# Two-layer attention and retention encoder on one core: other planner constants, nine written page orders, and another pair of operands cut by seven

## The chip, the cores and the metric

The kernel runs on one core of a Trainium2 chip. The time is the device time of one execution in microseconds (us), and lower is better. The profile is of one execution; its times are counted from the first instruction.

## What is computed

Each of two layers normalises the residual stream, multiplies it with one wide input matrix, runs grouped-query attention on half of the heads and two-way retention on the other half, and multiplies both with one output matrix:

```
DEPTH = 2; SEQ = 256; D_MODEL = 4096; IN_WIDTH = 11264
for l in range(DEPTH):
    h = rmsnorm(x, norm_w[l])
    aq, ak, av, ag, rq, rk, rv, rg = split(h @ w_in[l])          # 4096 x 11264
    a_out = silu(ag) * gqa_attention(rope(rmsnorm(aq)), rope(rmsnorm(ak)), av)
    r_out = silu(rg) * rmsnorm(bidirectional_retention(rope(rq), rope(rk), rv))
    x = x + concat(a_out, r_out) @ w_out[l]                      # 4096 x 4096
return rmsnorm(x, final_norm)
```

All of it is float32. The weights, 4096 by 11264 and 4096 by 4096 numbers in each layer, are read once.

## The kernel before

**Blocks and pairs.** The two big products are made in 30 blocks of 1024 output columns, numbered here 0 to 29 in the order in which they run: 11 of the first product of layer 0 (blocks 0 to 10), 4 of its second product (11 to 14), and the same for layer 1 (15 to 25, 26 to 29). A block runs over 4096 input channels as 16 pairs of 256 channels. For each pair the operand (256 tokens) is a 2 by 2 block matrix and so are the weights. An "eight" pair multiplies all eight quarter products. A "seven" pair uses the seven products of a fast 2 by 2 scheme, with sums of weight quarters (tile `wsum`) and sums of operand quarters (tile `xf`).

**Three matmuls for a product.** Float32 is kept by splitting each number into two rounded parts: ACT casts a weight page to `whi`, DVE subtracts to get `wlo`; operands are split likewise into `x8h`, `x8l` (eight pairs) and `x7h`, `x7l` (seven pairs). A product is then three matmuls of 128 by 128 by 512: high by high, high by low, low by high. An eight pair so costs 24 matmuls, a seven pair 21. Pairs 0 and 1 of block 0 are multiplied unsplit.

**Pages.** The weights of an eight pair come as two pages, A and B, those of a seven pair as four, A, T, B and U (T and U are made of sums). Rings of four `whi` and four `wlo` buffers hold pages ahead of TensorE, and six `wraw` buffers hold raw weights, loaded by the SP queue. A "far" page is loaded by the GpSimd queue straight into `fhi`; ACT negates it into `flo`, and a second, accumulating transfer adds the weights to that, so that DVE has nothing to do for it. By `FAR_PAIRS` page B of pairs 3, 6, 9, 12 and 15 is far, where the pair is an eight; in block 0 only from the third seven pair on.

**Which pairs are sevens.** `SEVEN` are sevens throughout, `AFTER` names pairs that become sevens from some block of a product on, one number for each layer. A pair that turns from eight to seven gets the missing operand sums in `sevenfold`, made between its last use in one block and its first use in the next. In the first two blocks (`PLAIN`) an eight pair uses an eighth PSUM bank; the operand differences that later blocks need (`third`, tile `x3f`) are made during blocks 0 to 2.

**The planner.** The program is written by a planner that runs when the kernel is built. It keeps a model of each engine's time (`Model`, with costs for each operation and `LATE`, the time until another engine sees a result) and gives the next instruction of DVE and ACT to whichever work, among what the model has ready within 0.02 us, has the earliest deadline less its own duration. A weight page's deadline is the modelled moment of its first matmul less `SLACK`. Everything else (operand splits, attention, retention, residual) runs in `Lane`s: an operand split is due `REST` before its first use, and other lanes follow two constants:

```python
return max(self.due, at + self.soft) if self.soft == SOFT else at + self.soft
```

Here `at` is now, `SOFT` is 5 us and `self.due` is the moment of the lane's creation plus `DUE`, 90 us. Some late tasks have `soft=URGENT` (0) and ignore `DUE`. The matmuls of attention and retention (PSUM tile `ps`) are put between the block's matmuls by `aside` once the model has their inputs ready for `PE_REST`. Once written, each engine's stream is fixed and runs in order.

Of the kernel before, what the change touches and what calls it, by code (L numbers as in the profile page):

```python
# [17 lines left out]
P = 128  # L18
# [28 lines left out]
DUE = 90.0  # L47

SOFT = 5.0
# [7 lines left out]
REST = 6.0  # L57
# [11 lines left out]
SEVEN = (0, 2, 5, 8, 11, 13)  # L69
# [3 lines left out]
AFTER = ({10: (3, 1)}, {10: (1, 1)})  # L73
# [11 lines left out]
MIX = False  # L85

GATE = 1

FAR_GAP = 0.0

SHIFT = 0.5
# [91 lines left out]

def in_groups(sevens, first=False):

    order = []
    for group in [tuple(range(_a, _b)) for _a, _b in zip(sevens, sevens[1:] + (NP,))]:
        one, rest = group[:1], group[1:]
        if first:
            order += [(_p, _k) for _p in NATIVE if _p in group for _k in (PAGE_A, PAGE_B)]  # L190
            one = [_p for _p in one if _p not in NATIVE]
            rest = [_p for _p in rest if _p not in NATIVE]
        one = [(_p, _k) for _p in one for _k in (PAGE_A, PAGE_T, PAGE_B, PAGE_U)]
        rest = [(_p, _k) for _p in rest for _k in (PAGE_A, PAGE_B)]
        for _v in one:
            order += [_v] + rest[:1]
            rest = rest[1:]
        order += rest
    return order


def evenly(sevens):

    order = []
    for _kind in (True, False):
        pages = [
            (_p, _k)
            for _p in range(NP)
            if (_p in sevens) == _kind
            for _k in ((PAGE_A, PAGE_T, PAGE_B, PAGE_U) if _kind else (PAGE_A, PAGE_B))  # L210
        ]
        order += [((_i + (SHIFT if _kind else 0.5)) / len(pages), _v) for _i, _v in enumerate(pages)]
    return [_v for _, _v in sorted(order)]


def pages_of(sevens, first=False):

    return in_groups(sevens, first) if first or not MIX else evenly(sevens)


def slots_of(sevens, first=False, plain=False):

    for _p, _k in pages_of(sevens, first):
# [20 lines left out]
LATE = {"V": 0.137, "A": 0.152, "P": 0.223, "G": 0.15}  # L244
# [243 lines left out]
def hybrid_encoder(  # L488
# [79 lines left out]
    def plan_of(l, second, b):  # L568
# [3 lines left out]
        plan.phase = 2 * l + 1 + second  # L572
        plan.start = (l, second, b) == (0, 0, 0)
# [5 lines left out]
        for slot in slots_of(plan.sevens, plan.start, plan.plain):  # L579
            flat += slot  # L580
# [25 lines left out]
    taken = [0]  # L606
# [83 lines left out]
    class Weights:  # L690


        def __init__(self):
            self.pages, at, far_after = [], 0, 0.0
            for plan in plans:
# [3 lines left out]
                for n, (name, p, _, k, h) in enumerate(plan.flat):  # L699
                    if (p, k) not in made:  # L700
# [4 lines left out]
                        at_page = cum[at + n]  # L705
                        one.far = not one.seven and not (start and (p < plan.sevens[2] or one.whole))
                        if FAR_GAP:
                            one.far = one.far and at_page >= far_after
                        else:
                            one.far = one.far and k == PAGE_B and p in FAR_PAIRS  # L710
                        if one.far:
                            far_after = at_page + FAR_GAP
# [63 lines left out]
        def due(self, g, low=False):  # L776
            return model.free["P"] + cum[g.first] - cum[done[0]] + (2 * MM * g.run if low else 0.0) - SLACK
# [207 lines left out]
    def split_pair(p, v, whole, stage):  # L985
# [44 lines left out]
        else:  # L1030
# [22 lines left out]
            if stage in DEFER:  # L1053
                if late is None or late > PLAIN:
                    thirds.append(Lane(third(p, *u, g)))
                    thirds[-1].pair = p
                    thirds[-1].use = plans[PLAIN].begins + next(i for i, v in enumerate(plans[PLAIN].flat) if v[1] == p)
# [76 lines left out]
    class Turn:  # L1134
# [21 lines left out]
        def soon(self, c):  # L1156
            return cum[first_use[self.stage + 1][2 * c]] - cum[done[0]] < AHEAD
# [34 lines left out]

    class Lane:
        def __init__(self, steps, heavy=True, need=0, own=0, owner=None, due=None, soft=None):
            self.need, self.own, self.owner = need, own, owner
            self.soft = SOFT if soft is None else soft
            self.steps, self.ops, self.begun, self.ended, self.then = steps, [], False, False, None
            self.due = clock["V"] + DUE if due is None else due
# [28 lines left out]
        def rested(self, at):  # L1227
# [7 lines left out]
            return ready + PE_REST <= max(at, free)  # L1235
# [367 lines left out]
    def retention_weights(L, i):  # L1603

        L.making = True
# [45 lines left out]
        L.weights[i], L.making = wT, False  # L1651
# [118 lines left out]
    def block(plan, after_pair, combine, then):  # L1770

        flat, order, plain, second = plan.flat, plan.order, plan.plain, plan.second
        first_order, last = plan.start, plan.last
# [292 lines left out]
    for i, L in enumerate(layers):  # L2066
        L.index = i
        L.rstd, L.kept, L.making = None, False, False
# [56 lines left out]
    for plan in plans:  # L2125
        l, L = plan.layer, layers[plan.layer]
        if not plan.second:
            bi = plan.b
            one = BLOCKS[bi][0]
            if one[0] == "rg":  # L2130
                tasks.append(Lane(retention_weights(L, one[1]), False, 3))
                tasks[-1].gate = lambda L=L, i=one[1]: not L.weights and (GATE < 1 or i // 2 in L.stored) and (GATE < 2 or not L.making)
# [92 lines left out]
```

## Time and profile before

| | |
|---|---|
| time, median of 3 runs | 2583.06 us (2581.98 to 2584.73) |
| time of the profiled execution | 2582.32 us |
| its span, first to last instruction | 2580.6 us |
| TensorE matmul, busy | 2565.2 us (99%) |
| TensorE weight load, busy | 2122.7 us (82%) |
| DVE, busy | 2340.3 us (91%) |
| ACT, busy | 1696.1 us (66%) |
| transfers | 690.75 MB, 268 GB/s |

A matmul's end in the profile is modelled and overlaps the next one, so a short wait of TensorE does not show as idle time; it is read from the distance between the starts of successive matmuls. 1.7 us of the profiled execution lie outside the span.

### The profile page before, as it was taken

The numbers are of one execution on the slowest core, as the hardware profiler recorded it, in microseconds if no ns is written. First come the engines' busy times: TensorE is split into PE (matmuls) and PEld (weight loads), VectorE is DVE, ScalarE is ACT, GpSimd is POOL, SyncE is SP. The second block draws the span as 40 slices with busy tenths as digits, with TensorE's granted clock in tenths as the row PEclk, the third lists the DMA queues.
The fourth block names the chain that finished last, engine by engine and source line by source line (L and its number), as shares of the span: only waits on it lengthen the run. The fifth ranks groups of instructions, "written<-read, shape, count | busy, mean of one in ns | idle before, by whom it ended". The sixth has DMA issues, their size and how long they took to land.

```text
span 2580.6 us, 34258 instructions
## 1 busy us (share of the span) xinstructions
PE 2565.2 (99%) x11491; PEld 2122.7 (82%) x11491; DVE 2340.3 (91%) x2939; ACT 1696.1 (66%) x2431; POOL 479.4 (19%) x694
## 2 busy tenths in 40 slices
PE   9999999999999999999999999999999999999998
PEld 7888888888888888888888888888888888888886
DVE  7999999889989999888899989999899899998887
ACT  7766766656665768555786666766666666775565
POOL 0211312211122111211121113212122112111111
PEclk9999999999999999999999999999999999999999
DMA  9998888878878887998998889898887887888896
GB/s 321 312 280 271 273 266 291 271 250 278 247 234 266 239 278 247 286 285 244 324 304 268 258 255 305 256 282 269 259 275 244 243 265 235 274 253 260 266 269 204
DMA packets 203858, 690.75 MB, mean 268 GB/s; under 512 B 24736, under 2 KB 31392, under 8 KB 203680
## 3 DMA queue, kind: packets, MB, share of 16 engines
q1 hardware_dynamic: 126304, 443.14, 48.0%
q0 software_dynamic: 77376, 245.41, 37.9%
q8 instruction: 90, 1.47, 0.2%
q14 instruction: 88, 0.72, 0.1%
HBM read 641.27 MB, written 47.19 MB: 267 GB/s over the span
## 4 chain that ended last, share of the span: by engine, by line
PE 96%; DVE 2%; DMA 1%; issue 1%; ACT 0%; POOL 0%; DVEq 0%; POOLq 0%; SPq 0%; ACTq 0%
PE M L421 92%; PE ps L421 4%; DVE wlo L421 1%; DMA flo<-in_w_in 1%; DVE cb L421 0%; DMA p_dram<-room 0%; DVE ca L421 0%; DMA full<-in_xT 0%; DVE wsum L421 0%; ACT ps L421 0%; DVE x8l L421 0%; ACT ca L421 0%; ACT tanh L421 0%; POOL p_dram L421 0%; DVE pTl L421 0%
## 5 line engine op out<-in xcount | busy, mean ns | idle before, releaser
L421 ACT CAST whi<-wraw 128x1024 fp32r<-128x1024 f32 (+1 forms) x807 | 753.5, 937 | 340.0 <-PE M L421 296.8
L421 DVE TENSOR_TENSOR wlo<-wraw,whi 128x1024 fp32r<-128x1024 f32 (+1 forms) x807 | 862.5, 1078 | 74.7 <-ACT whi L421 65.2
L421 ACT CAST whi<-wsum 128x1024 fp32r<-128x1024 f32 x406 | 426.2, 1050 | 257.4 <-PE M L421 157.6
L421 DVE TENSOR_TENSOR wlo<-wsum,whi 128x1024 fp32r<-128x1024 f32 x406 | 494.8, 1219 | 97.4 <-ACT whi L421 70.4
L421 PE MATMUL M<-whi,x7h 128*128 128x512 f32 x1465 | 570.7, 390 | 0.1
L421 PE MATMUL M<-whi,x7l 128*128 128x512 f32 x1465 | 570.4, 389 | 0.0
L421 PE MATMUL M<-wlo,x7h 128*128 128x512 f32 x1465 | 476.2, 389 | 0.0
L421 PE MATMUL M<-whi,x8l 128*128 128x512 f32 x1153 | 448.9, 389 | 0.1
L421 PE MATMUL M<-whi,x8h 128*128 128x512 f32 x1153 | 448.9, 389 | 0.0
L421 PE MATMUL M<-wlo,x8h 128*128 128x512 f32 x1153 | 355.6, 389 | 0.0
L421 PEld LDWEIGHTS M<-wlo,x7h 128*128 128x128 f32 x1465 | 274.9, 188 | 57.5 <-DVE wlo L421 0.3
L421 PEld LDWEIGHTS M<-whi,x7h 128*128 128x128 f32 x1465 | 275.1, 188 | 56.8 <-DVE cb L421 0.5
L421 PEld LDWEIGHTS M<-whi,x7l 128*128 128x128 f32 x1465 | 275.2, 188 | 56.4 <-issue 0.2
L421 ACT ACTIVATE flo<-fhi 128x1024 fp32r<-128x1024 f32 (+1 forms) x149 | 156.7, 1052 | 171.6 <-PE M L421 164.5
L421 PEld LDWEIGHTS M<-whi,x8h 128*128 128x128 f32 x1153 | 216.5, 188 | 45.4 <-DVE ca L421 0.5
L421 PEld LDWEIGHTS M<-whi,x8l 128*128 128x128 f32 x1153 | 216.5, 188 | 45.4 <-DVE x8l L421 0.6
L421 PEld LDWEIGHTS M<-wlo,x8h 128*128 128x128 f32 x1153 | 216.5, 188 | 45.1
L421 DVE TENSOR_TENSOR wsum<-wraw 128x1024 f32<-128x1024 f32 x203 | 247.0, 1217 | 4.8 <-DMA wraw<-in_w_in 2.7
L421 PE MATMUL M<-whi,x 128*128 128x512 f32 x728 | 224.3, 389 | 0.0
L421 POOL DMA_DIRECT2D fhi<-in_w_in x109 | 60.6, 556 | 875.7 <-PE M L421 871.9
L421 PE MATMUL M<-fhi,x8l 128*128 128x512 f32 x441 | 171.7, 389 | 0.0
L421 PE MATMUL M<-fhi,x8h 128*128 128x512 f32 x441 | 171.6, 389 | 0.0
(268 smaller groups left out, 3193.4 us busy)
## 6 DMA issues: line engine op xcount, KB each, us to landing
wraw<-in_w_in SPq DMA_DIRECT2D x591, 512.0 KB, 6.0
wraw<-in_w_out SPq DMA_DIRECT2D x216, 512.0 KB, 6.0
fhi<-in_w_in POOLq DMA_DIRECT2D x109, 512.0 KB, 5.2
flo<-in_w_in POOLq DMA_DIRECT2D x109, 512.0 KB, 8.5
fhi<-in_w_out POOLq DMA_DIRECT2D x37, 512.0 KB, 5.2
flo<-in_w_out POOLq DMA_DIRECT2D x37, 512.0 KB, 8.2
full<-next_dram POOLq DMA_DIRECT2D x24, 512.0 KB, 8.5
p_dram<-room POOLq DMA_DIRECT2D x64, 128.0 KB, 5.5
```

The costliest lines, as they stand in the source:

```text
L421: op.call()
```

## The change

Pair 5 leaves `SEVEN` and is listed in `AFTER`: in layer 0's first product it is an eight in block 0 and a seven from block 1 on, elsewhere a seven throughout. Pair 10, so far a seven from block 3 on in layer 0's first product, is one from block 1 on. `DUE` goes from 90 to 0 and `SOFT` from 5 to 7, so that a lane without a use is always due 7 us from now; `REST` goes from 6 to 9; the model's `LATE` becomes smaller. In nine blocks the order of pages is read from a table, `ORDERS` (a number is the pair, the letter its page), in place of `in_groups`. `FARS` sets the far pages of blocks 0, 7 and 18: pair 6 in block 0 (and by the rule on the third seven pair only 9, 12 and 15 are left there), pair 15 in block 7 and pair 9 in block 18 are no longer far. `SETS` overrides `SLACK` or `SOFT` in blocks 0, 8 and 23. Choices that were switched off (`MIX`, `FAR_GAP`) are removed.

```diff
-DUE = 90.0
-SOFT = 5.0
+DUE = 0.0
+SOFT = 7.0
...
-REST = 6.0
+REST = 9.0
...
-SEVEN = (0, 2, 5, 8, 11, 13)
+SEVEN = (0, 2, 8, 11, 13)
 MORE = ()
-AFTER = ({10: (3, 1)}, {10: (1, 1)})
+AFTER = ({5: (1, 0), 10: (1, 1)}, {5: (0, 0), 10: (1, 1)})
...
+ORDERS = {
+    2: '0A 0T 1A 1B 0B 2A 3A 2T 0U 3B 2B 4A 2U 4B 5A 6A 5T 5B 6B 7A 5U 7B 8A 9A 8T 9B 8B 8U 10A 10T 10B 10U 11A 12A 11T 12B 11B 13A 14A 11U 13T 14B 13B 13U 15A 15B',
...
+    23: '0A 0T 1A 1B 0B 3A 0U 2A 2T 3B 2B 4A 2U 4B 6A 5A 5T 6B 5B 7A 5U 7B 8A 9A 8T 9B 8B 8U 10A 10T 10B 10U 11A 12A 11T 12B 11B 11U 13A 14A 13T 14B 13B 13U 15A 15B',
+}
+FARS = {
+    0: '3B 9B 12B 15B',
+    7: '3B 6B 9B 12B',
+    18: '3B 6B 12B 15B',
+}
+SETS = {
+    (0, 'SLACK'): 0.0,
+    (8, 'SOFT'): 5.0,
+    (23, 'SOFT'): 5.0,
+}
...
-LATE = {"V": 0.137, "A": 0.152, "P": 0.223, "G": 0.15}
+LATE = {"V": 0.11, "A": 0.112, "P": 0.198, "G": 0.15}
...
+        plan.index = l * (N_IN + N_OUT2) + second * N_IN + b
+        plan.fars = parsed(FARS[plan.index]) if plan.index in FARS else [(p, PAGE_B) for p in FAR_PAIRS]
...
+        pages = parsed(ORDERS[plan.index]) if plan.index in ORDERS else in_groups(plan.sevens, plan.start)
+        for slot in slots_of(pages, plan.sevens, plan.start, plan.plain):
...
         def deadline(self, at):
             if self.use is not None:
-                return model.free["P"] + cum[self.use] - cum[done[0]] - REST
-            return max(self.due, at + self.soft) if self.soft == SOFT else at + self.soft
+                return model.free["P"] + cum[self.use] - cum[done[0]] - setting("REST", REST)
+            if self.soft is None:
+                return max(self.due, at + setting("SOFT", SOFT))
+            return at + self.soft
```

`ORDERS` holds blocks 2, 3, 4, 8, 15, 18, 19, 22 and 23.

## Rows read from the trace of the kernel before

**Rows 1.** The page's head: busy us, share of the span and instructions of each engine.
```profile
PE 2565.2 (99%) x11491; PEld 2122.7 (82%) x11491; DVE 2340.3 (91%) x2939; ACT 1696.1 (66%) x2431; POOL 479.4 (19%) x694
```
**Rows 2.** The chain that ended last, in order of time: start, us, what.
```profile
173.99 63.92 PE M L421 x282
...
2048.28 92.51 PE M L421 x408
```
**Rows 3.** Timeline 17 to 31 us: start, us, instruction, idle before it and releaser.
```profile
19.49 0.79 PE L421 MATMUL M<-whi,x7h 128*128 128x512 f32 x1
...
20.12 0.40 PE L421 MATMUL M<-whi,x7l 128*128 128x512 f32 x1
...
28.81 0.39 PE L421 MATMUL M<-whi,x8h 128*128 128x512 f32 x1
...
29.34 0.19 PEld L421 LDWEIGHTS M<-whi,x8l 128*128 128x128 f32 x1 [0.57 <-DVE x8l L421]
```
**Rows 4.** Timeline 90 to 96 us, the turn from block 0 to block 1.
```profile
94.33 0.39 PE L421 MATMUL M<-wlo,x7h 128*128 128x512 f32 x1
...
94.81 0.19 PEld L421 LDWEIGHTS M<-whi,x7h 128*128 128x128 f32 x1 [0.52 <-DVE cb L421]
```
**Rows 5.** Timeline of PE, 611 to 613 us, early in block 7.
```profile
611.43 0.62 PE L421 MATMUL M<-whi,x 128*128 128x512 f32 x2
612.29 0.51 PE L421 MATMUL ps<-pTl,kv 128*128 128x512 f32 x1 [0.24 <-DVE pTl L421]
```
**Rows 6.** Timeline of PE, 975.5 to 978.5 us, in block 11.
```profile
975.96 0.28 PE L421 MATMUL ps<-vh,wTh 128*128 128x256 f32 x1
976.48 0.39 PE L421 MATMUL ps<-vl,wTh 128*128 128x256 f32 x1 [0.25 <-DVE vl L421]
976.71 0.28 PE L421 MATMUL ps<-vh,wTl 128*128 128x256 f32 x1
976.83 0.28 PE L421 MATMUL ps<-vh,wTh 128*128 128x256 f32 x1
...
977.37 0.28 PE L421 MATMUL ps<-vh,wTl 128*128 128x256 f32 x1
```
**Rows 7.** Timeline of PE, 1450.5 to 1453.5 us, late in block 16.
```profile
1450.95 0.61 PE L421 MATMUL M<-fhi,x 128*128 128x512 f32 x2
1452.93 0.50 PE L421 MATMUL M<-flo,x 128*128 128x512 f32 x1 [1.37 <-DMA flo<-in_w_in]
```
**Rows 8.** The accumulating transfers into flo: issue to landing, last line of that tile's view.
```profile
DMA to landing us min/median/max: 4.0/8.4/13.3
```
**Rows 9.** Blocks 0, 1, 2, 3, 7: stretch, length, busy us of each engine, clock, transfers.
```profile
6.00:93.20 87.20, 87.01 (x354) 66.36 (x355) 74.38 (x106) 72.05 (x129) 6.38 (x9) 1.00 0.98 345
93.20:176.50 83.30, 83.20 (x367) 68.62 (x366) 81.10 (x134) 53.31 (x79) 22.85 (x23) 1.00 0.95 285
176.50:261.70 85.20, 85.20 (x385) 70.87 (x385) 81.17 (x110) 55.71 (x85) 14.69 (x21) 1.00 0.84 260
261.70:349.10 87.40, 87.40 (x394) 72.56 (x393) 81.15 (x97) 59.84 (x93) 21.12 (x33) 1.00 0.89 283
...
609.10:696.30 87.20, 86.96 (x388) 71.76 (x388) 82.02 (x97) 54.62 (x65) 14.51 (x22) 1.00 0.83 251
```
**Rows 10.** DVE's groups in block 1: count, busy us, mean ns of one, idle before.
```profile
L421 DVE TENSOR_TENSOR wlo<-wraw,whi 128x1024 fp32r<-128x1024 f32 x21 | 25.3, 1214 | 0.0
...
L421 DVE TENSOR_TENSOR wsum<-wraw 128x1024 f32<-128x1024 f32 x6 | 7.3, 1214 | 0.0
L421 DVE TENSOR_TENSOR wsum<-wraw,wsum 128x512 f32<-128x512 f32 x7 | 4.8, 680 | 0.0
```
**Rows 11.** The operand sums, tile xf: duration ns min/median/max, first and last start.
```profile
L421 DVE TENSOR_TENSOR x7l<-xf,x7h x28: 806/815/826, 10.7 to 2312.8; 128x640 fp32r<-128x640 f32 x28
...
L421 DVE TENSOR_TENSOR xf<-full x24: 275/281/284, 9.4 to 2293.3; 128x128 f32<-128x128 f32 x24
...
L421 DVE TENSOR_TENSOR xf<-x7h,x7l x4: 681/683/684, 240.1 to 2306.8; 128x512 f32<-128x512 f32 x4
```

More of the change, by code (lines that the diff above doesn't have):

```diff
@@ L181, in sevens_of, with parsed @@
     return tuple(sorted({*SEVEN, *(MORE if second else ()), *late}))
+def parsed(text):
+    return [(int(_v[:-1]), "ATBU".index(_v[-1])) for _v in text.split()]
 def in_groups(sevens, first=False):
@@ L199, in in_groups, with slots_of @@
     return order
[L202 to L223, printed above, removed]
+def slots_of(order, sevens, first=False, plain=False):
+    for _p, _k in order:
         if _p in sevens and not (first and _p in NATIVE):
@@ L605, in hybrid_encoder @@
             cum.append(cum[-1] + MM * (WHOLE if plan.start and v[1] in NATIVE else 3))
-    taken = [0]
+    taken, playing = [0], [0]
     nw = t(cp, [P, DEPTH * (KT + KT // 2)], "nw")
@@ L693, in __init__ @@
         def __init__(self):
-            self.pages, at, far_after = [], 0, 0.0
+            self.pages, at = [], 0
             for plan in plans:
@@ L704, in __init__ @@
                         one.seven = p in plan.sevens and not one.whole
[L705 to L712, printed above, removed]
+                        one.far = (p, k) in plan.fars and not one.seven and not (start and (p < plan.sevens[2] or one.whole))
                         one.kept = None
@@ L776, in due @@
         def due(self, g, low=False):
-            return model.free["P"] + cum[g.first] - cum[done[0]] + (2 * MM * g.run if low else 0.0) - SLACK
+            return model.free["P"] + cum[g.first] - cum[done[0]] + (2 * MM * g.run if low else 0.0) - setting("SLACK", SLACK)
         def ready(self, e, ins, old=None):
@@ L1056, in split_pair @@
                     thirds[-1].pair = p
-                    thirds[-1].use = plans[PLAIN].begins + next(i for i, v in enumerate(plans[PLAIN].flat) if v[1] == p)
+                    plan = plans[stage // 2 * (N_IN + N_OUT2) + PLAIN]
+                    thirds[-1].use = plan.begins + next(i for i, v in enumerate(plan.flat) if v[1] == p)
             else:
@@ L1156, in soon @@
         def soon(self, c):
-            return cum[first_use[self.stage + 1][2 * c]] - cum[done[0]] < AHEAD
+            return cum[first_use[self.stage + 1][2 * c]] - cum[done[0]] < setting("AHEAD", AHEAD)
         def step(self):
@@ L1191, in free_bank, with setting @@
         do(partial(bank.__setitem__, 0, False))
+    def setting(name, value):
+        return SETS.get((playing[0], name), value)
     class Lane:
@@ L1195, in __init__ @@
             self.need, self.own, self.owner = need, own, owner
-            self.soft = SOFT if soft is None else soft
+            self.soft = soft
             self.steps, self.ops, self.begun, self.ended, self.then = steps, [], False, False, None
-            self.due = clock["V"] + DUE if due is None else due
+            self.due = clock["V"] + setting("DUE", DUE) if due is None else due
             self.pair = self.use = None
@@ L1234, in rested @@
             model.free["P"] = free
[L1235 removed]
+            return ready + setting("PE_REST", PE_REST) <= max(at, free)
         def deadline(self, at):
             if self.use is not None:
[L1239 to L1240 removed]
+                return model.free["P"] + cum[self.use] - cum[done[0]] - setting("REST", REST)
+            if self.soft is None:
+                return max(self.due, at + setting("SOFT", SOFT))
+            return at + self.soft
     def spawn(steps):
@@ L1650, in retention_weights @@
         yield
-        L.weights[i], L.making = wT, False
+        L.weights[i] = wT
         own(-2)
@@ L2067, in hybrid_encoder @@
         L.index = i
-        L.rstd, L.kept, L.making = None, False, False
+        L.rstd, L.kept = None, False
         L.tables, L.weights, L.rs, L.stored = {}, {}, {}, {}
@@ L2131, in hybrid_encoder @@
                 tasks.append(Lane(retention_weights(L, one[1]), False, 3))
-                tasks[-1].gate = lambda L=L, i=one[1]: not L.weights and (GATE < 1 or i // 2 in L.stored) and (GATE < 2 or not L.making)
+                tasks[-1].gate = lambda L=L, i=one[1]: not L.weights and i // 2 in L.stored
             if bi == N_IN - 1:
```

7 lines of the change are left out of this document (1 added, 6 removed), and 7 rows, old and new, of the table ORDERS.

## The prediction

> **What bounds the kernel now.** I read the head of the page first: TensorE's matmuls are busy for 99% of the span, DVE for 91%, ACT for 66% [rows 1]. Matmul ends are modelled, so a busy share of 99% could still hide waits. The chain that ended last settles it: it runs for long stretches through matmuls alone, 282 of them in 63.92 us and 408 in 92.51 us [rows 2], which is 0.2267 us for each, early and late in the kernel. In these stretches nothing but the number of matmuls sets the time. So the time is that of a matmul stream plus the places at which the stream breaks, and I looked for each break as a distance between two starts that is longer than 0.2267 us (0.12 us for the 256-column matmuls of retention, as from 976.71 to 976.83 [rows 6]).
>
> The breaks of some size are these. In block 0 a matmul at 19.49 is followed by one at 20.12, which is 0.40 us too late, and one at 28.81 by a weight load at 29.34 that waited for an operand split on DVE, 0.30 us [rows 3]. At the turn to block 1 TensorE waits for DVE to empty a PSUM bank, 0.25 us [rows 4]. In block 7 two matmuls at 611.43 are followed by an attention product at 612.29 that waited for DVE: 0.86 less 0.45, so 0.41 us [rows 5]. In block 11 five retention matmuls between 975.96 and 977.37 take 1.41 us where 0.60 would do: 0.81 us [rows 6]. In block 16 an accumulating transfer is late: from 1450.95 to 1452.93 two matmuls take 1.98 us, 1.53 us too long [rows 7]. That transfer is an exception, since the median of its kind lands in 8.4 us and the slowest took 13.3 [rows 8]. The sum is 0.40 + 0.30 + 0.25 + 0.41 + 0.81 + 1.53 = 3.70 us. This is all that better planning can win between the kernel's start and its tail, 0.14% of 2583. A gain of more than 0.2% (5.2 us, about what a measurement of this kernel can tell from no change) is out of its reach by itself.
>
> **The change, part by part.** *Matmuls.* A product is three matmuls, and a seven pair has one product fewer. Pair 5 as an eight in block 0 adds one product; pair 10 as a seven in blocks 1 and 2 removes two. Everywhere else the sets are as before. Net: three matmuls fewer, 3 x 0.2267 = 0.68 us, and the PE count goes from 11491 [rows 1] to 11488.
>
> *DVE's work for weights.* By the groups of block 1 [rows 10], a seven pair costs DVE three sums (1.21 + 0.68 + 0.68) and four low parts (3 x 1.21, and a half page taken like the half sums, 0.68), 6.9 us; an eight pair costs two low parts, 2.4 us. So each switch is 4.5 us of DVE. Block 0 loses 4.5 us for pair 5 and gains 1.2 us for page B of pair 6, which is no longer far. Blocks 1 and 2 gain 4.5 us each. In block 1 two pairs need `sevenfold` during the block turn, each one sum of 0.68, four of 0.28 and a low part of 0.82 [rows 11], 2.6 us; that of pair 10 came at the end of block 2 before. Block 1 gains 4.5 + 5.2 = 9.7 us. DVE was busy there for 81.10 of 83.30 us [rows 9], so 2.2 us were free, and the block becomes 0.68 us shorter: 9.7 - 2.2 + 0.7 = 8.2 us of DVE work must be done elsewhere or TensorE waits. Blocks 2 and 3 had 4.0 and 6.3 us free [rows 9] and block 0 has 12.8 plus the 3.3 that it loses. Block 2's 4.5 is offset by the 2.6 that it no longer does. What can be moved out of block 1 is what has no use in it: the tables, keys and values of attention, and the operand differences (`third`), which are first used in block 2. I left out that pair 10 no longer needs its `third`, so 8.2 is an upper bound. Between 0 and 8.2 us I take 0: the free time of the neighbours, 10.3 us after the block alone, exceeds it, and the lanes concerned have no use in the block. Without that cover it costs the 8.2.
>
> *Far pages.* Besides pair 6, one page in block 7 and one in block 18 become near pages: 1.2 us of DVE each, ACT as before (a cast in place of a negation), one 512 KB transfer less. In block 7 DVE has 5.2 us free [rows 9], which hides it; without cover it costs at most 1.2 us a block. I take 0.
>
> *Deadlines.* `DUE`, `SOFT`, `REST`, `SLACK` and `LATE` add no instruction. They change which of DVE's and ACT's waiting pieces goes first. Until now a fresh lane yielded to every weight page for 90 us; now it goes ahead of any page that is needed more than 7 us later. Weight pages so stand closer to their use, and what is queued behind a lane's instruction is the next `whi` or `wlo`, for which TensorE waits. The gain side: attention and retention parts are ready earlier when their matmuls come, and operand splits, due 9 us ahead in place of 6, come earlier. The two breaks in block 0 are a page and a split of the start, where `SLACK`, `FARS` and `REST` all change, and the turn to block 1 has 3.3 us less DVE work before it: I take these 0.95 us as gone (bounds 0 and 0.95). The breaks in blocks 7, 11 and 16 lie in blocks without a written order; two wait on lane work that moves, one on a transfer that was slow once. I take half of their 2.75 us, 1.38 (bounds 0 and 2.75).
>
> *New breaks.* Eleven blocks get another order or another set of pairs (the nine written ones and blocks 0 and 1). The trace of before has no row for these orders. The nearest row is the breaks that planned blocks have now: 3.70 us over 30 blocks, 0.12 us a block, so 11 x 0.12 = 1.36 us. The lower bound is 0. The upper one is the 8.2 us above.
>
> Sum on the profiled execution: 2582.32 - 0.68 - 0.95 - 1.38 + 1.36 = 2580.7 us. The median of the runs is 0.74 us above that execution, so the median forecast is **2581.4 us**, 0.06% less than before.
>
> **The rivals.** *Breaks only move.* DVE has some 2 to 6 us free in each of these blocks [rows 9], so work cannot go much earlier than it does, and `DUE` does little of what it says; the breaks are as many as before and only the three matmuls count: 2583.06 - 0.68 = 2582.4 us. For it: the largest break is a single slow transfer. Against it: three of the breaks are in blocks 0 and 1, whose DVE work changes.
>
> *All breaks go.* 2583.06 - 0.68 - 3.70 = 2578.7 us. Against it: one of them is a transfer that no deadline makes faster, and every new order can bring its own.
>
> *DVE becomes the bound in block 1 (slower).* If the 8.2 us cannot leave the block, TensorE waits for `wlo`, or for a PSUM bank that DVE has not emptied, as at the turn before it [rows 4]: 2583.06 - 0.68 + 8.2 = 2590.6 us with the old breaks kept. It decides from 5.9 us of waits on. For it: DVE's 97% there, the highest of the first blocks. Against it: the free time beside it.
>
> *Early lanes stand in the way (slower).* An instruction of attention or retention that is put early into DVE's or ACT's stream and whose input is late holds up everything behind it, weight pages too. The trace prices one such wait: 0.41 us in block 7 and 0.81 in block 11 [rows 5, 6], 0.61 on average. With eight attention groups and eight retention pairs of one or two waits each there are some 32 places; a third of them, 11, would cost 6.7 us: 2583.06 - 0.68 + 6.7 = 2589.1 us. From ten such waits on it is slower by over 0.2%. For it: pages are only 7 us ahead. Against it: the planner gives out only what its model has ready within 0.02 us, and of these 32 places two wait now. The Trainium skill (TensorE: Matmul & The Clock Gate, Architectural detail on the array) says that TensorE can pull weight loads ahead while ACT and DVE are strictly first in, first out; by that rule each late input costs its whole wait, and the two rows agree in that TensorE stood still behind DVE there.
>
> **How the numbers follow.** Chances: the forecast 0.52, breaks only move 0.25, all breaks go 0.10, DVE bound 0.07, early lanes in the way 0.06. All but the last two end within 0.2% (2577.9 to 2588.2). Faster by over 0.2% needs more than all breaks, so a shorter start or tail or a lucky median: 0.05, taken from the case of all breaks gone. The two slow cases give 0.13 slower, and 0.82 is left within. The range goes from 2578.0, just below all breaks gone, to 2587.0, where 4.7 us of new waits, over half of the 8.2, stand beside old breaks that stay: some 0.15 is left out.
>
> **What would show it.** Right: 11488 PE instructions; no DVE release of TensorE between 19 and 96 us; stretches of the chain at 0.2267 us for a matmul; starts in blocks 1 to 3 without distances over some 0.5 us; DVE near 100% in block 1 and fuller in block 2. Wrong if TensorE waits for `wlo`, `cb` or `ca` in blocks 1 to 3 by microseconds, if `ps` matmuls wait in many blocks, or if transfers into `flo` are late more often, since loads now start later behind later splits.

## The result, and the profile after

The changed kernel takes 2590.3 us (median of 6 runs, 2587.42 to 2592.99) beside 2581.32 us of the kernel before on the same chip (6 runs, 2578.68 to 2584.73). The ratio is 1.0034, with a 95% interval from 1.0021 to 1.0047. So it is slower by 9.0 us, and the forecast of 2581.4 us (range to 2587.0) was wrong in sign and size. (It started from a median of 2583.06 us in three runs; with six runs the kernel before is 1.7 us faster, so what was forecast is 1.65 us faster and what came is 9.0 us slower.) A second set of runs of the same kernel, below, gave 2588.68 us and 1.0032. The profiled execution took 2587.42 us, its span 2585.6; it is the fastest of the six.

The head of the page, which answers to [rows 1]:

```profile
PE 2567.5 (99%) x11488; PEld 2123.5 (82%) x11488; DVE 2349.3 (91%) x2944; ACT 1698.5 (66%) x2432; POOL 468.8 (18%) x688
```

Three matmuls are gone, as forecast, and still PE is 2.3 us longer busy. The shares are the old ones: this view does not show the loss. The chain that ended last still has long stretches of matmuls alone; they answer to [rows 2]:

```profile
990.29 331.20 PE M L423 x1461
...
2269.58 292.89 PE M L423 x1292
```

331.20 / 1461 is 0.2267 us, the old pace. So the loss lies again in breaks. TensorE's view of waits names what ended each kind (us in total, how often, the longest), first for the kernel before:

```profile
PE M L421 <- DMA flo<-in_w_in: 1.4, 1, 1.4
...
PE ps L421 <- DVE vl L421: 0.2, 1, 0.2
PE ps L421 <- DVE pTl L421: 0.2, 1, 0.2
```

and for the changed kernel:

```profile
PE M L423 <- DVE cb L423: 2.3, 1, 2.3
...
PE M L423 <- DMA flo<-in_w_in: 0.9, 1, 0.9
PE ps L423 <- DVE aql L423: 0.7, 2, 0.4
PE M L423 <- DVE wlo L423: 0.4, 1, 0.4
PE ps L423 <- DVE pTl L423: 0.4, 1, 0.4
```

The late transfer has shrunk; what is new are waits for DVE: for the emptying of a PSUM bank (`cb`), for a weight's low part (`wlo`), and for the operand splits of attention (`aql`, `pTl`).

**The turn to block 1**, which was forecast to lose its break. PE's timeline, answering to [rows 4]:

```profile
94.84 0.39 PE L423 MATMUL M<-wlo,x7h 128*128 128x512 f32 x1
97.49 0.50 PE L423 MATMUL M<-whi,x7h 128*128 128x512 f32 x1 [2.26 <-DVE cb L423]
```

From start to start it is 2.65 us, 2.43 too long; before it was 0.25. DVE's own timeline says why. In the kernel before, the last bank of block 0 (`cb<-cb,ps`) was emptied at 94.68 to 95.28, and DVE had stood idle for 1.27 us before a `wsum` at 86.54. In the changed kernel:

```profile
90.14 0.81 DVE L423 TENSOR_TENSOR x7l<-xf,x7h 128x640 fp32r<-128x640 f32 x1
...
94.94 0.68 DVE L423 TENSOR_TENSOR cb<-cb,M 128x512 f32<-128x512 f32 x1
95.54 0.17 DVE L423 TENSOR_SCALAR ls<-ls 128x32 f32<-128x32 f32 x1
95.63 1.21 DVE L423 TENSOR_TENSOR wsum<-wraw 128x1024 f32<-128x1024 f32 x1
96.76 0.67 DVE L423 TENSOR_TENSOR cb<-cb,M 128x512 f32<-128x512 f32 x1
97.36 0.68 DVE L423 TENSOR_TENSOR cb<-cb,ps 128x512 f32<-128x512 f32 x1
```

An operand split of a new seven pair (0.81) stands ahead of the combining (`cb`, `ca`: the adding up of the banks, which empties them), and between two emptyings of banks stand a small piece and a sum of the next block's weights (95.54 to 96.76, 1.22 us). DVE is full there, and TensorE takes the delay whole. It also pays a second time, as the windows show (stretch, length, busy us of each engine, granted clock, DMA share, GB/s):

```profile
94.80:97.50 2.70, 0.44 (x3) 0.01 (x2) 2.70 (x6) 0.21 (x1) 0.88 (x1) 1.00 0.86 278
97.50:99.00 1.50, 1.50 (x4) 1.20 (x5) 1.50 (x3) 0.57 (x2) 0.00 (x0) 0.63 0.96 235
99.00:101.00 2.00, 2.00 (x6) 1.57 (x5) 2.00 (x4) 1.28 (x3) 1.04 (x2) 0.50 0.90 164
```

After the wait the granted clock falls to half, 1.2 in place of 2.4 GHz, and matmuls start 0.43 us apart (99.04, 99.47, 99.89) until 101.17. Seven are 0.20 us late each and the ones beside them in part, 1.7 us in all.

**An operand split behind weight work**, in block 6, whose set of pairs and page order are unchanged. PE, then DVE, then ACT:

```profile
583.66 0.40 PE L423 MATMUL ps<-pTh,kv 128*128 128x512 f32 x1
584.46 0.50 PE L423 MATMUL ps<-pTl,kv 128*128 128x512 f32 x1 [0.40 <-DVE pTl L423]
```
```profile
581.45 1.22 DVE L423 TENSOR_TENSOR wlo<-wraw,whi 128x1024 fp32r<-128x1024 f32 x1
582.58 0.68 DVE L423 TENSOR_TENSOR wsum<-wraw,wsum 128x512 f32<-128x512 f32 x1
583.18 1.22 DVE L423 TENSOR_TENSOR pTl<-pT,pTh 128x1024 fp32r<-128x1024 f32 x1
```
```profile
580.36 1.06 ACT L423 CAST pTh<-pT 128x1024 fp32r<-128x1024 f32 x1 [0.72 <-DMA pT<-p_dram]
```

`pTh` is there at 581.42, after waiting 0.72 us for its own load. `pTl` could follow at once, but DVE does a low part and a sum of weights first and takes it up at 583.18; the product that needs it is due 0.24 us after 583.66 and starts at 584.46. Here it is not an early piece that stands in the way of a page (the rival of early lanes) but a page that stands in the way of a piece with no time left.

**The end.** From the last matmul's start to the end of the span it is 12.44 us, and was 11.80. No computation is later: SP's last issues, first before, then after, stand 7.82 and 7.80 us behind the last matmul (2568.75 and 2573.18).

```profile
2576.57 0.59 SPq L421 DMA_DIRECT2D out<-cb  x1
```
```profile
2580.98 0.60 SPq L423 DMA_DIRECT2D out<-cb  x1
```

From there to the end of the span it is 4.0 us before and 4.6 after: the last output transfers land 0.65 us later. The forecast had no term for this.

**The balance.** For each matmul I took the distance to the next start less the pace of its own shape (0.2267 us for 512 columns), and summed that from 21 us (behind the pages of the start that are multiplied in another way) to the last matmul. That is the lost time of the tables below.

| us | before | before, again | after | after, again |
|---|---|---|---|---|
| span | 2580.55 | 2581.10 | 2585.62 | 2585.64 |
| TensorE's lost time | 6.71 | 7.59 | 12.09 | 11.57 |
| last matmul's start to the end | 11.80 | 11.81 | 12.44 | 12.45 |

For the first pair: 12.09 - 6.71 = 5.38, less 0.68 for three matmuls, plus 0.64 at the end, is 5.34 of the 5.07 us by which the span is longer; the rest, -0.27, lies ahead of 21 us. In the second pair it is 3.98 - 0.68 + 0.64 = 3.94 of 4.54, and the rest is +0.60.

### The profile page after: what moved, and what is told of

Read it like the earlier page. It is cut to its first block, busy times and chain, and to the rows that moved or that the text cites. A ratio compares the mean times of both kernels' runs of the same rounds, so it can differ in the third digit from the quotient of the medians.

```text
span 2585.6 us, 34263 instructions
## 1 busy us (share of the span) xinstructions
PE 2567.5 (99%) x11488; PEld 2123.5 (82%) x11488; DVE 2349.3 (91%) x2944; ACT 1698.5 (66%) x2432; POOL 468.8 (18%) x688
## 4 chain that ended last, share of the span: by engine, by line
PE 95%; DVE 2%; issue 1%; DMA 1%; ACT 1%; POOL 0%; SPq 0%; DVEq 0%; POOLq 0%; ACTq 0%
PE M L423 91%; PE ps L423 4%; DVE wlo L423 1%; DMA flo<-in_w_in 0%; DVE wsum L423 0%; ACT whi L423 0%; DVE cb L423 0%; DMA p_dram<-room 0%; DVE ca L423 0%; DMA fhi<-in_w_in 0%; ACT pr L423 0%; DVE rot L423 0%; ACT ps L423 0%; DVE aql L423 0%; DVE x7l L423 0%
## 5 line engine op out<-in xcount | busy, mean ns | idle before, releaser
L423 ACT CAST whi<-wsum 128x1024 fp32r<-128x1024 f32 x408 | 428.3, 1050 | 278.8 <-DVE wsum L423 125.3
```

The source lines that it names most:

```text
L423: op.call()
```

## The experiments

Eighteen runs follow, two of them of the two kernels unchanged. The theories, A to C and F to I, are named in the expectations; none carries the loss alone, as will be seen. Below, "new deadlines" are `DUE` 0 and `SOFT` 7, "old deadlines" 90 and 5.

**One part undone.** The LATE of before (`e1_late`), the deadlines of before (`e2_due`), the sets of before, which needs block 2's order removed (`e3_pairs`), and no written orders (`e4_orders`):

```
-LATE = {"V": 0.11, "A": 0.112, "P": 0.198, "G": 0.15}
+LATE = {"V": 0.137, "A": 0.152, "P": 0.223, "G": 0.15}
```
```
-DUE = 0.0
+DUE = 90.0
-SOFT = 7.0
+SOFT = 5.0
```
```
-SEVEN = (0, 2, 8, 11, 13)
+SEVEN = (0, 2, 5, 8, 11, 13)
-AFTER = ({5: (1, 0), 10: (1, 1)}, {5: (0, 0), 10: (1, 1)})
+AFTER = ({10: (3, 1)}, {10: (1, 1)})
```
```
+ORDERS = {}
```

> The changed kernel with the old, longer LATE in the planner's model, all else as changed. Theory A (the first turn: the new pair sets and page orders put too much DVE work around the turn from block 0 to block 1, where TensorE waits 2.4 us for a PSUM bank and then runs at half clock): no help, 2588 to 2591 us. Theory B (cushion: lanes that are due in 7 us and a model that thinks results arrive sooner leave everything closer to its use, so each late transfer or operation shows): about half of the loss comes back, 2584 to 2587 us, and the attention matmuls wait less. Theory C (the nine written orders are at fault): no help, 2588 to 2591 us.

> The changed kernel with DUE back at 90 and SOFT at 5 us. Theory A: little help, 2587 to 2590 us, since the lanes of the first turn have uses of their own. Theory B: most of the loss comes back, 2582 to 2585 us. Theory C: no help, 2588 to 2591 us.

> The changed kernel with the old pair sets (pair 5 a seven throughout, pair 10 a seven from block 3 of layer 0), for which block 2 loses its written order. Theory A: the 2.4 us wait at the turn to block 1 and the some 1.6 us of half clock after it go, against 0.7 us for three more matmuls: 2586 to 2588 us. Theory B: 2589 to 2592 us. Theory C: 2588 to 2591 us.

> The changed kernel without any written order: all blocks by in_groups. Theory A: no help at the first turn, 2589 to 2592 us. Theory B: 2589 to 2592 us or worse, since no cushion comes back. Theory C: 2582 to 2585 us, and the waits in the nine blocks go.

| run | median us (range) | ratio to before [95%] | TensorE's lost time, us |
|---|---|---|---|
| e1_late | 2590.72 (2585.35 to 2591.79) | 1.0032 [1.0019, 1.0044] | 10.4 |
| e2_due | 2600.4 (2598.98 to 2604.73) | 1.0078 [1.0064, 1.0092] | 29.4 |
| e3_pairs | 2587.41 (2584.84 to 2588.95) | 1.0022 [1.0013, 1.0032] | 12.9 |
| e4_orders | 2588.97 (2586.67 to 2590.3) | 1.003 [1.0018, 1.0041] | 12.4 |

Undoing a part does not give its share back. The sets are worth 1.3 to 2.9 us by the changed kernel's two medians, with ranges that overlap (A, in part): the wait at the turn to block 1 is gone in that profile, but 2.3 us for the transfer into `flo` in block 15 stand there instead, so the profile's lost time is no lower. LATE and the orders give nothing that can be told from no change (C is weak); with the old LATE the turn loses 0.25 us only, but two splits `pTl`, at 570 and 1862 us, are 1.7 us late each. The deadlines of before make it much slower, and the waits say where:

```profile
PE M L423 <- ACT ca L423: 9.5, 3, 7.2
```

With the new LATE and the old deadlines the bank that the first matmul of block 7 needs is emptied 7.2 us late. The same 7.2 us wait appears when LATE alone is put on the kernel before (next group), and not in the changed kernel. With the old deadlines block 7 so depends on LATE, and, as the next group shows, on the sets too.

**One part alone, on the kernel before.** The new sets (`e6_b_pairs`), deadlines (`e7_b_due`), LATE (`e8_b_late`), and REST 9 in place of 6 (`e12_b_rest`): the diffs above the other way round, and

```
-REST = 6.0
+REST = 9.0
```

> The kernel before with the new pair sets alone. Theory A: slower by 2.5 to 4 us, 2584.5 to 2586 us, with a wait of over 1 us at the turn to block 1. Theory B: 0.7 us of matmuls fewer and no new wait, 2580.5 to 2582 us.

> The kernel before with DUE 0 and SOFT 7 alone. Theory A: within 2 us of before, 2580 to 2584 us. Theory B: slower by 4 to 7 us, 2586 to 2589 us, with attention matmuls (ps) that wait for DVE in the first product of both layers.

> The kernel before with the new, shorter LATE alone. Theory A: within 2 us of before, 2580 to 2584 us. Theory B: slower by 1 to 4 us, 2583 to 2586 us, with more waits of 0.1 to 0.5 us spread over the kernel.

> The kernel before with REST 9 in place of 6 alone, by which the sums of x begin some 4 us earlier. Theory F: somewhat slower, 2582 to 2585 us, with a later turn. Theory A: within 1.5 us of before, 2579.5 to 2582.5 us.

| run | median us (range) | ratio to before [95%] | lost time, us |
|---|---|---|---|
| e6_b_pairs | 2593.32 (2590.46 to 2596.01) | 1.0046 [1.0031, 1.0061] | 17.1 |
| e7_b_due | 2597.64 (2595.25 to 2604.62) | 1.0072 [1.0054, 1.0091] | 19.6 |
| e8_b_late | 2621.06 (2618.84 to 2624.08) | 1.0155 [1.014, 1.017] | 43.3 |
| e12_b_rest | 2581.47 (2579.72 to 2583.71) | 1.0003 [0.9994, 1.0012] | 5.7 |

The first three cost 12, 17 and 40 us; all together, with the orders, cost 7 to 9. So the parts do not add up, and the changed kernel is better than any of its larger parts alone. The new sets alone do not do what A said: at the turn to block 1 `e6_b_pairs` has no break over 0.25 us. Of its 17.1 us 10.9 are lost around the start of block 7, where TensorE waits 4.2 us for ACT's piece of attention `pr` and 2.7 us for a bank (`ca`), and half clock follows. The new deadlines alone make the late splits that B foretold, 3.3 us before `pTl` and 2.0 us before `aql`, at a cost well over B's. REST changes nothing that can be measured.

**A suspected wait taken away.** At the turn, block 0's combining due 3.7 us earlier (`e5_turn`). In the changed kernel ACT waited 1.88 us at 57.68 for a load of the input's rows, with weight work behind it, so the sums over these rows were held back (`e9_hold58`). Last, on top of that, the inputs of lanes' products ready 5 us ahead in the three blocks with late splits (`e10_psrest`):

```
-            return model.free["P"] + cum[n.begins + min(uses)] - cum[done[0]] - 0.3 if uses else at + SOFT
+            return model.free["P"] + cum[n.begins + min(uses)] - cum[done[0]] - (4.0 if plan.start else 0.3) if uses else at + SOFT
```
```
     def first_sums():
+        while model.free["P"] < 58.0:
+            yield
```
```
 SETS = {
+    (3, 'PE_REST'): 5.0,
+    (6, 'PE_REST'): 5.0,
+    (17, 'PE_REST'): 5.0,
```

> The changed kernel, where the work that empties the PSUM banks of block 0 gets a deadline 3.7 us earlier, so that DVE does it ahead of weight pages at the first turn; nothing else differs before that. Theory A: the 2.4 us wait of TensorE at the turn and the half clock behind it go (no wait over 0.6 us between 90 and 104 us, granted clock 1.00 in 98 to 101), and the time falls by some 3 us to 2586 to 2588 us. Theory B: the wait only moves, to a low part that is late instead, and the time stays at 2589 to 2591 us.

> The changed kernel, where the sums of squares of x (eight loads of 512 KB and sixteen ACT operations, first_sums) may not begin before 58 us of the planner's time, as late as they began before the change. Theory F (early lanes in the way of an in-order engine): the wait at the first turn comes from here. ACT waits 1.9 us for the first x at 57 us, a weight cast stands behind it, DVE's low part behind that, and DVE is full until the turn. Held back, no ACT wait for x over 1 us between 50 and 66 us, no TensorE wait over 0.8 us between 90 and 104 us, clock 1.00 there, and 2.5 to 4 us less than the changed kernel. Theory A (the load of the new pair sets): the turn still waits 2 us or more, 2589 to 2591 us.

> As the run with the sums held back, and in blocks 3, 6 and 17 attention's matmuls are put into TensorE's stream only when the planner has their inputs ready for 5 us in place of 3. Theory F: the waits of ps matmuls at 330, 583 and 1506 us (0.6, 0.7 and 0.9 us in the profile) go, a further 1.5 to 3 us. Theory G (DVE is simply behind there, whatever waits for it): the ps waits go, but as much appears at low parts nearby, and the time stays within 1 us of the run with the sums held back.

| run | median us (range) | ratio to before [95%] | lost time, us |
|---|---|---|---|
| e5_turn | 2588.12 (2584.91 to 2592.25) | 1.0026 [1.0017, 1.0036] | 10.3 |
| e9_hold58 | 2589.83 (2588.51 to 2593.81) | 1.0038 [1.0025, 1.0051] | 17.1 |
| e10_psrest | 2589.63 (2588.33 to 2592.84) | 1.0035 [1.0022, 1.0047] | 12.3 |

Each did what it was to do and won nothing that the intervals show. In `e5_turn` the turn's wait fell from 2.43 to 1.02 us, and it was now one for a low part (`wlo`), as its rival B expected. In `e9_hold58` it was gone, but a transfer into `flo` in block 1 was 3.9 us late, and half clock followed; F, the theory that this early lane is what costs, fell. In `e10_psrest` the late splits at 331 and 1507 us were gone, but the third that was aimed at, before the same matmul of block 6, at 585 us, grew to 1.5 us, and splits were late in block 21, where nothing was edited (0.4 to 0.6 us at 1848 and 1864). G's time came true; its waits at low parts nearby were not what took their place.

**Both kernels again.** Is what a profile shows the plan's or the execution's? The changed kernel (`e11_again`) and the kernel before (`e16_before`), unchanged:

> The changed kernel once more, for a second profile. If the wait at the first turn and the waits of attention's matmuls are the plan's, they stand at the same matmuls again, within some 0.5 us each; what is a slow transfer's shows once. Median 2588 to 2592 us.

> The kernel before, unchanged, for a second profile. If the breaks that the prediction counted belong to its order of work, the same matmuls wait again near 611, 976 and 1451 us, with sums of waits of 6 to 7 us after 19.4 us. Rival: they belong to one execution, above all the late transfer near 1451 us, which is then gone, and the sum is 5.5 us or less.

`e11_again` took 2588.68 us (2587.42 to 2592.37), 1.0032 [1.002, 1.0044]; `e16_before`, one run, 2582.88. Of the changed kernel's waits these come in both profiles, in us: the start at 28.5 (0.38 and 0.40), `pTl` at 583.7 (0.56, 0.59), `wlo` at 591.2 (0.57, 0.58), `flo` at 1342.6 (1.03, 1.26), `aql` at 1506.7 (0.52, 0.65). They belong to the order of work. The turn's wait is there twice but is 2.43 in one and 0.67 in the other, with the same order on DVE. Others over 0.4 us come once: 0.45 at 330.6 in the first; 0.95 at 425.4 (`aql`), 0.54 at 566.2 (`pTl`) and 0.58 at 1871.0 in the second, places of the same few kinds.

The kernel before shows in its second profile the wait at the turn (0.33) and the transfer in block 16, now 2.11 us too long, and neither the break at 611 us nor that at 976 [rows 5, 6]. So those two were one execution's, and the one that the prediction called an exception [rows 7] is the plan's; `e12_b_rest` shows it too, with 1.76. After this wait in `e16_before` the clock fell also:

```profile
1449.50:1451.50 2.00, 0.21 (x1) 0.00 (x0) 2.00 (x3) 0.00 (x0) 0.00 (x0) 1.00 1.06 387
...
1453.00:1456.00 3.00, 3.00 (x9) 2.33 (x9) 1.28 (x2) 0.00 (x0) 0.00 (x0) 0.57 0.53 190
```

**Pages given back their distance.** Theory B: lanes that go first leave weights nearer to their use. The measure is ACT's idle time before the casts of sums, by what ended it, in the groups of instructions of the kernel before, the changed kernel and `e13_due22`:

```profile
L421 ACT CAST whi<-wsum 128x1024 fp32r<-128x1024 f32 x406 | 426.2, 1050 | 257.4 <-PE M L421 157.6 <-DVE wsum L421 81.7 <-issue 8.6
```
```profile
L423 ACT CAST whi<-wsum 128x1024 fp32r<-128x1024 f32 x408 | 428.3, 1050 | 278.8 <-DVE wsum L423 125.3 <-PE M L423 116.8 <-issue 21.3
```
```profile
L467 ACT CAST whi<-wsum 128x1024 fp32r<-128x1024 f32 x408 | 428.3, 1050 | 256.5 <-PE M L467 132.8 <-DVE wsum L467 99.2 <-issue 12.9
```

In the kernel before ACT mostly waits for TensorE to give buffers back (157.6 us): it is ahead. In the changed kernel it mostly waits for DVE's sums (125.3): DVE is behind. The old deadlines were put back in 22 blocks (all but 5 to 8 and 20 to 23, where the 7.2 us wait arose), the written order of block 15 was taken out, and both:

```
 SETS = {
+    (0, 'DUE'): 90.0,
+    (0, 'SOFT'): 5.0,
...
+    (29, 'DUE'): 90.0,
+    (29, 'SOFT'): 5.0,
```
```
 ORDERS = {
-    15: '0A 0T 1A 1B 0B 0U 2A 3A 2T 3B 4A 2B 2U 4B 5A 6A 7A 5T 5B 6B 5U 7B 8A 9A 8T 9B 8B 10A 10B 8U 11A 12A 11T 12B 11B 11U 13A 14A 13T 14B 13B 13U 15A 15B',
```

> The changed kernel with the kernel before's yielding of lanes to weight pages (DUE 90, SOFT 5) in 22 of its 30 blocks; blocks 5 to 8 and 20 to 23 keep DUE 0 and SOFT 7. Theory B (lanes that go first leave weight pages and operand splits nearer to their use): the idle time of ACT before whi sums that waits for DVE's wsum falls from about 127 us to 100 us or less, the waits of TensorE after 19.4 us fall from about 12 us to 9 or less, and the time is 2583 to 2587 us. Rival G (deadlines are not it; the new sets and orders leave DVE behind anyway): ACT's wait stays at 120 us or more and the time is 2588 to 2591.

> The changed kernel without the written order of block 15, every other block's order kept. If that order by itself causes the late accumulating transfer near 1342 us, the wait of 1.0 to 1.3 us there goes and the time falls by about that, to 2587.5 to 2589. Rival: a transfer that is late for contention comes back at another page, and the time stays within 0.5 us of the changed kernel's 2589.5.

> Both edits: DUE 90 and SOFT 5 in the same 22 blocks, and no written order for block 15. Theory B with the order of block 15: the gains of the two runs add up, 2582 to 2586 us, waits of TensorE after 19.4 us at 8 us or less. Rival G: 2587 to 2590 us, waits at 10 us or more.

| run | median us (range) | ratio to before [95%] | lost time, us |
|---|---|---|---|
| e13_due22 | 2590.8 (2588.08 to 2595.65) | 1.004 [1.0028, 1.0053] | 14.3 |
| e14_no15 | 2587.05 (2585.55 to 2588.46) | 1.0022 [1.0012, 1.0032] | 11.5 |
| e15_both | 2592.57 (2587.8 to 2593.9) | 1.0044 [1.003, 1.0058] | 15.8 |

ACT's wait for DVE's sums fell to 99.2 us as B foretold, and the time did not fall: pages had their distance back, and TensorE now waited longer for the splits of attention.

```profile
PE ps L467 <- DVE pTl L467: 4.1, 3, 2.7
```

But these three waits, at 576.0, 600.1 and 1853.5 us, lie in blocks 6 and 21, which kept the new deadlines. In the 22 blocks that got the old ones back TensorE lost 4.0 us (8.7 and 6.9 in the changed kernel's two profiles, 4.6 and 5.8 in the kernel before's), in the eight others 10.4 (3.4 and 4.7; 2.1 and 1.8). So this run does not refute B: where the old deadlines stood again the loss was gone, and it grew where the new ones stayed. Why it grew there is not shown.

Block 15's late transfer needs its written order: without it the wait of 1.03 to 1.26 us is gone and 0.56 us for a cast stand there. Of the nine profiles with that order seven have the wait (0.87 to 2.30 us), of the eleven without it none. But `e5_turn` and `e13_due22` keep the order and lose 0.3 us at most in the whole block, so it is not enough by itself. The median is 1.6 us lower than in `e11_again`, with ranges that overlap. The two edits do not add up: `e15_both` is 5.5 us slower than `e14_no15`.

**Several parts undone together.** From `e14_no15` on, the old sets and the old LATE (`e17_pairs_late`), then also the old deadlines in the same 22 blocks (`e18_three`):

> The changed kernel with the old sets of pairs, the old LATE, and no written orders for blocks 2 and 15; the new deadlines (DUE 0, SOFT 7) and REST 9 stay. Three matmuls more (0.68 us) than the changed kernel. If the sets and LATE together make most of the loss, the waits of TensorE after 19.4 us fall to 8.5 us or less, attention's ps matmuls wait 1 us or less in all, and the time is 2583 to 2585.5 us. Rival H (the deadlines make ps and weight waits by themselves): ps waits stay at 2 us or more and the time is 2586 to 2589.

> As e17_pairs_late, and in addition DUE 90 and SOFT 5 in 22 blocks; left of the change are seven written orders, REST 9, the near pages and the new deadlines in blocks 5 to 8 and 20 to 23. If sets, LATE and deadlines together are the loss, and each alone only moves it, the time comes back to the kernel before: 2581 to 2584 us, waits after 19.4 us at 8 us or less, ACT's wait for wsum under 95 us. Rival I (any other order of work than the kernel before's costs 4 us or more, whatever its constants): 2585 to 2589 us.

| run | median us (range) | ratio to before [95%] | lost time, us |
|---|---|---|---|
| e17_pairs_late | 2597.38 (2593.35 to 2600.67) | 1.0063 [1.005, 1.0076] | 21.3 |
| e18_three | 2586.3 (2584.78 to 2588.84) | 1.002 [1.0011, 1.0029] | 10.1 |

```profile
PE ps L421 <- DVE pTl L421: 5.8, 3, 2.5
PE M L421 <- DMA flo<-in_w_in: 2.7, 1, 2.7
```
```profile
PE M L465 <- DMA flo<-in_w_in: 1.2, 1, 1.2
PE M L465 <- DVE cb L465: 1.1, 1, 1.1
```

The first block is `e17_pairs_late`, the second `e18_three`. With old sets and old LATE the new deadlines cost 11 us (2597.38 against 2586.3), where with the new sets and LATE it is their undoing that costs, by the medians 0.5 to 2.1 us (`e13_due22`) and 5.5 (`e15_both` against `e14_no15`). H is right on the mechanism there: with the old LATE the new deadlines make more late splits, 7.8 us lost before `pTl` and `aql` (1.9 and 3.1 in the changed kernel); its time, 2586 to 2589 us, was 8 too low. And `e18_three`, which keeps seven written orders, REST, `SLACK` 0 in block 0, near pages and the new deadlines in eight blocks, is still 5 us slower than the kernel before. That is in the range of I, that another order of work costs some 4 us whatever the constants, but it does not show I: `e12_b_rest` is an exception, and the eight blocks of new deadlines stayed.

**All twenty profiles side by side.** Sorted by the deadlines that a block was planned with, three kinds of breaks over 0.25 us separate, in us:

| | old deadlines in that block | new deadlines in that block |
|---|---|---|
| block 6, before `pTl` | none in 6 profiles | 0.3 to 2.7 in each of 14 |
| block 16, late transfer into `flo` | 1.2 to 2.4 in each of 9 | none in 11 |
| start of block 7, a bank late by 3 or more | 3 of 6 profiles | none in 14 |

Over the whole kernel, TensorE loses 0 to 0.7 us before `pTl` and `aql` in the six profiles with old deadlines throughout, and 1.9 to 7.8 in the eleven with new ones throughout. Two pairs differ in the deadlines alone: `e7_b_due` loses 7.2 us there and the kernel before 0.4 and 0.2; `e2_due` loses 0.7 and the changed kernel 1.9 and 3.1. So the late splits are the work of the new deadlines, whatever the sets, orders and LATE; in exchange the late transfer of block 16 is gone. The old deadlines escape the stall of block 7 in the kernel before and `e12_b_rest`, and not with the new LATE or the new sets.

## Why the prediction was wrong

**The step that failed** is "New breaks": "Eleven blocks get another order or another set of pairs", 11 x 0.12 = 1.36 us. Both factors were too small. The deadlines, which "add no instruction", were costed only for old breaks that they might close. But they set the order of DVE's and ACT's work in every block. Comparing the order of DVE's instructions in the two traces (the longest sequence common to both), 28% of 2939 stand elsewhere: some 24 to 47% in each of the 24 blocks 0 to 11 and 15 to 26, 2 to 9% in the six others. Blocks 6 and 17, where three of the recurring waits are, have neither a new order of pages nor a new set, and 35% and 24% of DVE's instructions stand elsewhere there. What they cost the runs show: the late splits before `pTl` and `aql`, 1.9 and 3.1 us in the two profiles in place of 0.4 and 0.2, come and go with the deadlines. The second factor came from the breaks of a plan whose order had been chosen with these breaks in sight, which a new order has not. The breaks over 0.25 us that the prediction left in its sum were 3.70 - 0.95 - 1.38 + 1.36 = 2.73 us; the changed kernel's are 6.3 us and 1.7 us of half clock in the first profile, 7.2 us in the second. That is 8.0 - 2.7 = 5.3 of the 6.7 us by which the profiled execution missed the sum (2587.42 against 2580.7); 0.64 us is the end, and the remaining 0.8 us, shorter delays and the start, were not taken apart.

**Old breaks.** The 0.95 us of block 0 and the turn were wrong: the break of 0.40 us near 19.5 is in every profile of every kernel, the one at 28.8 stayed, and the turn grew. The 1.38 us for blocks 7, 11 and 16 came out as a gain of all three, but two of them had been one execution's, which the prediction could have told only from a second profile, so of those two the gain is luck; the late transfer of block 16, "a transfer that no deadline makes faster", went with the old deadlines, and another came in block 15.

**Matmuls.** Right: 11488, and the pace of 0.2267 us.

**DVE's work in block 1.** The windows of blocks 0 to 3, cut at the changed kernel's own boundaries, answer to [rows 9]:

```profile
6.00:93.70 87.70, 87.48 (x356) 66.36 (x355) 74.89 (x112) 73.97 (x137) 6.61 (x8) 1.00 0.97 345
93.70:180.20 86.50, 84.24 (x365) 69.26 (x364) 84.14 (x131) 51.84 (x73) 16.43 (x22) 0.98 0.92 271
180.20:265.40 85.20, 85.20 (x389) 70.98 (x387) 82.99 (x111) 58.91 (x93) 17.04 (x25) 1.00 0.88 260
265.40:353.30 87.90, 87.61 (x394) 72.61 (x393) 80.41 (x96) 59.95 (x94) 19.61 (x29) 1.00 0.86 270
```

DVE has 3.0 us more in block 1, not 9.7, and 1.8 more in block 2. The 5.2 us for the two pairs' operand sums and splits never fell into block 1: their first pieces start at 57.9 and 70.2 us and the last split at 90.14, all in block 0, which so has 0.5 us more DVE work where 3.3 less were forecast. Apart from the turn, block 1 has no large wait. Yet block 1 is 3.2 us longer, and all of it is the turn (2.43 - 0.25 us of wait and 1.7 of half clock, less the 0.68 of the matmuls). So "DVE becomes the bound in block 1" named the right engine, the right releaser (`cb`) and the right place, "a PSUM bank that DVE has not emptied, as at the turn"; the price of 8.2 us was too high, and `e3_pairs` puts what the sets cost at 1.3 to 2.9 us by the medians. But the sets are not what sets the wait there. `e6_b_pairs` has them and no wait; `e17_pairs_late` and `e18_three` have the old ones, and the turn loses 1.6 and 1.3 us, since a low part stands between two emptyings of banks. From `e17_pairs_late`:

```profile
94.20 0.68 DVE L421 TENSOR_TENSOR cb<-cb,M 128x512 f32<-128x512 f32 x1
94.80 1.22 DVE L421 TENSOR_TENSOR wlo<-wraw,whi 128x1024 fp32r<-128x1024 f32 x1
95.93 0.68 DVE L421 TENSOR_TENSOR cb<-cb,M 128x512 f32<-128x512 f32 x1
```

As far as these timelines show, what matters is which piece of weight work the planner puts there, and how far behind DVE then is: with one and the same order the turn lost 2.43 and 0.67 us.

**Early lanes in the way.** Its 6.7 us are near to what happened, by another mechanism. What waits in the shown place is not a page behind an early lane but a lane's split behind a page, and holding back the one early lane that had pages behind it (`e9_hold58`) won nothing. What both share is the rule of the Trainium skill that the prediction weighed (TensorE: Matmul & The Clock Gate, Architectural detail on the array): DVE takes its instructions strictly in order. The trace agrees at 581.45 to 583.18 us, where `pTl` waits behind a low part and a sum although its own input is there.

**What stays open.** The profiles show 4.5 to 5.1 us; the medians, each against the kernel before on its own chip, differ by 6.9 to 9.0. The profiles of the changed kernel are both the fastest of their runs, those of the kernel before are not, so some 2 to 4 us are in executions that no trace shows. And why the kernel before and `e12_b_rest`, in which 6% of DVE's instructions stand elsewhere, lose 6 to 8 us, and every other kernel here 10 or more, was not isolated: the share that moves does not say it (`e6_b_pairs` moves 10% and loses 17 us, `e18_three` 20% and 10 us). Two kernels that could have told were not run: the kernel before with the written orders alone, and `e18_three` with the old deadlines in all thirty blocks. No run beat the kernel before.

## What to carry to other kernels

Where one engine paces a kernel and a second one is 91% busy, in a fixed order, changing a priority or a due time is not free: it reorders the second engine everywhere, so count the blocks whose order changes, not those that the diff names, and price new breaks from a plan that was not chosen for having few. Settings of such a plan work as a set: each of the three larger parts taken over alone, and the deadlines undone alone, was worse than the whole here (LATE alone cost 40 us, all together 7 to 9). Where a setting can be chosen block by block, read the waits of the blocks that got it apart from the others': the time of `e13_due22` hid that the loss was gone where its edit was made. And take a second profile before you count small breaks: two of the six largest here were one execution's, and the one that looked like an accident was the plan's.

## What the runs showed of the hardware

A wait of TensorE can cost more than itself: after idle times of 2.26 us (turn to block 1) and 1.95 us (block 16, `e16_before`), with PE busy before them, the granted clock fell to half (0.50 in the window 99 to 101, and 0.57 as the mean of 1453 to 1456, which reaches past its end) for the next 3 us or so and matmuls started 0.43 us apart, which cost 1.7 us more each time. The length of the wait does not decide it alone: after 1.37 us in [rows 7] the clock stayed at 1.00, and so it did after idle times of 2.24 us (`e15_both`, 1457 us), 2.32 (`e10_psrest`, 130 us) and 2.65 (`e17_pairs_late`, 131 us). The output transfers at the end took 0.65 us longer from SP's last issue to the end in both profiles of the changed kernel, though the issues stood equally far behind the last matmul; with the old LATE put back it is 12.1 us from the last matmul to the end (`e1_late`), yet the new LATE alone on the kernel before leaves it at 11.8 (`e8_b_late`), and why was not looked into.
